# A two-layer hybrid encoder in fp32: the first FFN stage's down projection by seven products, the residual in one tile, and three token tiles added to it by one accumulating DMA

## The chip, the cores and the metric

The kernel is one program on one NeuronCore of a Trainium2 chip. The metric is the device time of one execution in microseconds (us); the median of several runs is given. The profile is one execution seen by the hardware profiler. The engines are TensorE (PE: matmuls; PEld: its weight loads), VectorE (DVE), ScalarE (ACT), GpSimd (POOL) and SyncE (SP, which here only issues DMAs). GpSimd issues DMAs too, on a software queue of its own.

## The reference

Two token sequences (512 and 256 tokens, together 768 = 6 tiles of 128, model width 1024) go through two layers. Each layer has a half-step SwiGLU FFN, a mixer, and a second half-step FFN:

```python
def swiglu(x, wg, wu, wd):
    return (jax.nn.silu(x @ wg) * (x @ wu)) @ wd
...
x = x + 0.5 * swiglu(rms_norm(x, norm_ffn[layer, 0]), w_ffn_gate[layer, 0],
                     w_ffn_up[layer, 0], w_ffn_down[layer, 0])
hn = rms_norm(x, norm_mix[layer])
# even layer: z = hn @ w_in_even, a state-space scan and neighbourhood attention, @ w_out_even
# odd layer:  z = hn @ w_in_odd, windowed grouped attention, @ w_out_odd
x = x + 0.5 * swiglu(rms_norm(x, norm_ffn[layer, 1]), ...)
```

The FFN's inner width is 2816 = 22 chunks of 128. All data are fp32. The result is `rms_norm(x, norm_final)` of both sequences.

## The kernel before

The program has six stages in a row: FFN 0 (until about 565 us), the even mixer (until 890), FFN 1 (until 1383), FFN 2 (until 1875), the odd mixer (until 2150) and FFN 3. The residual x lives in SBUF all along, in six tiles of 128 tokens x 1024 (`self.x`).

**Precision.** Each fp32 matrix is held as a high and a low part; a product is the three matmuls high x high, high x low and low x high. A weight tile `raw` comes by a DMA of SP (L80); ScalarE casts its high part (L89), VectorE subtracts it to get the low part (L90), both into a tile `whl`, of which there are seven.

**An FFN stage.** The 22 chunks are taken in 11 pairs b. For a pair, gate and up projections are done over a 2 x 2 split (two chunks, two halves of the tokens) by seven products of sub-matrices and sums of them instead of eight (Strassen and Winograd); each product is 12 matmuls of 128x384 (`prod`, L283). Beside block b, the down projection of block b-1 is woven in (`woven`). In stages 1 to 3 it goes by seven products too (`down`): 7 x 9 matmuls of 128x512 (L391), each giving three token tiles of one 512-wide half of x. Six of seven products are evacuated by ScalarE into a tile y (L398) and added to x by an accumulating DMA that GpSimd issues (L399), one for each token tile; the product of quadrant (1,0), and one tile more, are added by VectorE (L395). In stage 0 the down projection is `plain`: 12 steps of 6 matmuls (L469), added to x by VectorE (L416). The last block of every stage is plain (`step`, L457), and there the next norm begins, token tile by token tile (L217 to L232, transposes L1269).

**Sums for the seven products.** In stages 1 to 3 the hidden tiles `h` are also combined to s1 to s4, each with a cast on ScalarE and a subtraction on VectorE. Stage 0 needs none of them (`last` is true there for every block).

**The state-space preparation** runs beside stage 0 (`extra`, one step after each product from block 2 on): it turns the scan's parameters into matrices in DRAM (W1d, W2d, Ed) for the even mixer. First VectorE works out powers (L558 to L655). Then there are 16 rounds, one for each pair of groups: `start` runs a chain of some 20 GpSimd operations (L677 to L700), `finish` stores W2 (L706), transposes w1 on TensorE (four transposes, L711, and small matmuls, L718 to L722), ScalarE copies the transposed tile to `w1e` (L712), and `store` writes it to W1d (L729) and a small tile to Ed (L730). The chain's scratch (n1, n2, m1, m2) lies in the same memory as `w1e`, so the next chain's first operation (L677) waits until the store to W1d has landed. At the end SP gathers Md from Ed (L744).

All instructions of an engine run in program order, as do the DMAs of one queue; the framework sets semaphore waits where tiles overlap.

Of the kernel before, what the change touches and what calls it, by code (L numbers as in the profile page):

```python
# [12 lines left out]
F32 = mybir.dt.float32  # L13
F32R = mybir.dt.float32r
I32 = mybir.dt.int32
AF = mybir.ActivationFunctionType
ALU = mybir.AluOpType
# [3 lines left out]
P = 128  # L21
# [26 lines left out]
class Trunk:  # L48
    def __init__(self, ctx, tc, a, y_p, y_s):
# [12 lines left out]
        self.one = warm  # L62
        self.x = [self.xp.tile([P, DM], F32, name=f"x{t}", tag=f"x{t}") for t in range(6)]
        self.queue = deque()
# [33 lines left out]
    def weights(self):  # L98
# [62 lines left out]
        def fast(q):  # L161
            both = ("w_gate", "w_up")
            first = [quad(n, q, 0) for n in both]
            for z in first * 2 + [head(n, q, 1) for n in both] * 2 + first * 5:
                yield next(z)
            for b in range(1, NF // 2):
                pair = [quad(n, q, b, b == 1) for n in both]
                if q == 0:
                    yield from chain(pair[0], plain(q, b - 1), pair[1])
                else:  # L170
                    yield from woven(b, chain(*pair), down(q, b - 1))
            yield from plain(q, NF // 2 - 1)
# [85 lines left out]
    def ffn(self, q, norm, tail, extra=None):  # L258
# [5 lines left out]
        with ExitStack() as ctx:  # L264
# [9 lines left out]
            def ct():  # L274
                return fp.tile([P, H], F32, tag="ct", name="ct", bufs=5)

# [70 lines left out]
            def up(b):  # L347

                last = b == NF // 2 - 1 or q == 0
                sums = {}  # L350
# [28 lines left out]
            def down(b):  # L379
# [4 lines left out]
                def step(h, w, bank, first, i, j):  # L384
                    w = self.take("w_down", q, b, w)
                    for n in range(3):
                        if first:
                            z[bank, n] = self.ps()
                        o = z[bank, n]
                        for m, (a, c) in enumerate(((0, 0), (1, 0), (0, 1))):  # L390
                            nc.tensor.matmul(o, hs[h][:, c, n * P : (n + 1) * P], w[:, a], start=first and m == 0, stop=m == 2,  # L391
                                             skip_group_check=True)
                        xs = self.x[TILES[3 * i + n]][:, j * 512 : (j + 1) * 512]
                        if (i, j) == (1, 0) or (i, j, n) == (0, 0, 0):
                            v.scalar_tensor_tensor(xs, o, 0.5, xs, ALU.mult, ALU.add)  # L395
                        else:
                            y = fp.tile([P, 512], F32, tag="y", name="y", bufs=5)
                            nc.scalar.activation(y, o, AF.Copy, scale=0.5)  # L398
                            nc.gpsimd.dma_start(xs, y, accum_op=ALU.add)  # L399

# [3 lines left out]
                    ("s4", "22", "c", False, 0, 1))]  # L404

            def plain(b):

                st = {}

                def step(e, n):  # L410
                    if n == 0:
                        st["w"] = [self.take("w_down", q, 2 * b + f, e) for f in range(2)]
                    o = self.ps()
                    self.rows(o, act, n, st["w"])
                    xs = self.x[TILES[n]][:, e * 512 : (e + 1) * 512]
                    v.scalar_tensor_tensor(xs, o, 0.5, xs, ALU.mult, ALU.add)  # L416

                return [lambda e=e, n=n: step(e, n) for e in range(2) for n in range(6)]

# [17 lines left out]
            for b in range(1, NF // 2):  # L437
                g, u = (z[2:] for z in (g1, u1)) if b == 1 else pair(b)
                for s in g + plain(b - 1) + u if q == 0 else woven(b, g + u, iter(down(b - 1))):
                    s()  # L440
                    if b > 1:
                        next(extra, None)
# [73 lines left out]
    def s5_matrices(self, pool, spare):  # L516
# [148 lines left out]
        def start(q):  # L665
# [10 lines left out]
            for r in range(2):  # L676
                gp.tensor_mul(n1[:, r], b[:, r], crb)  # L677
                gp.tensor_mul(n2[:, r], b[:, 1 - r], cib)
            yield
            gp.tensor_sub(bb[:, 0, :2], n1[:, 0], n2[:, 0])  # L680
# [19 lines left out]
            gp.tensor_add(w1[:, :, 1], m1, m2)  # L700
            yield

# [739 lines left out]
```

## Time and profile before

| | before |
|---|---|
| median of 3 runs | 2641.98 us (2640.18 to 2642.34) |
| the profiled execution's own time | 2640.13 us |
| its span in the trace | 2638.3 us |
| busy share of the span: PE, DVE, ACT, POOL | 98%, 76%, 59%, 29% |
| moved by DMA | 342.92 MB, mean 130 GB/s |

A busy share is that of the whole span and mixes stages with different limits. The span is what the trace covers; the run's own time is 1.8 us longer, and the median of the other runs 1.85 us above that.

### The profile page before, as it was taken

Reading aid. Unit: us, or ns where it says so; the run is one execution under the profiler, and the core shown is the slowest. Engines: PE = TensorE matmul, PEld = TensorE weight load, DVE = VectorE, ACT = ScalarE, POOL = GpSimd, SP = SyncE. Lnnn points to the kernel's source line nnn. Section 1 sums busy time; section 2 is a strip of 40 time slices with the busy share of each in tenths; the row PEclk is TensorE's granted clock in tenths of the full one; section 3 lists DMA queues with packets and bytes.
Section 4 is the critical chain, followed back from the end, with each engine's and each line's share of the span. In section 5 each row is a group of like instructions: output and inputs, shape, how many; then the busy total and the mean of one; then the engine's idle time right before and its main releaser. Section 6 shows DMA issues by size and latency. Waiting matters only on the chain.

```text
span 2638.3 us, 40405 instructions
## 1 busy us (share of the span) xinstructions
PE 2595.2 (98%) x14370; PEld 2344.0 (89%) x14370; DVE 2015.5 (76%) x3925; ACT 1545.2 (59%) x3202; POOL 769.1 (29%) x1191
## 2 busy tenths in 40 slices
PE   8999999999999999999999999999999999999998
PEld 7999899888787899999998999999887789999997
DVE  8977777564864888787879878787647788878786
ACT  6334334354564666666667666666558766666665
POOL 0255655302820033333321323232100003333332
PEclk9999999999999999999999999999999999999999
DMA  4223223326243277777755877777401127777775
GB/s 154 71 90 104 78 91 104 106 74 155 82 155 108 88 168 165 171 166 170 167 108 137 190 169 167 168 170 148 128 17 41 65 88 168 165 171 166 170 167 129
DMA packets 145661, 342.92 MB, mean 130 GB/s; under 512 B 25265, under 2 KB 32385, under 8 KB 145202
## 3 DMA queue, kind: packets, MB, share of 16 engines
q0 software_dynamic: 74032, 139.01, 29.3%
q1 hardware_dynamic: 71426, 201.33, 23.7%
q8 instruction: 113, 1.85, 0.3%
q14 instruction: 90, 0.74, 0.1%
HBM read 198.65 MB, written 17.89 MB: 82 GB/s over the span
## 4 chain that ended last, share of the span: by engine, by line
PE 73%; DVE 4%; ACT 2%; DMA 1%; issue 1%; POOL 0%; DVEq 0%; ACTq 0%; POOLq 0%
PE ps L283 33%; PE ps L391 16%; PE ps L255 9%; PE ps L487 5%; PE ps L469 2%; PE ps L1111 1%; DVE whl L90 1%; PE ps L1099 1%; PE ps L1130 1%; DMA x<-y 1%; DVE raw L232 1%; PE ps L920 1%; PE ps L855 1%; PE ps L819 1%; PE ps L883 1%
## 5 line engine op out<-in xcount | busy, mean ns | idle before, releaser
L90 DVE TENSOR_TENSOR whl<-raw,whl 128x512 fp32r<-128x512 f32 x856 | 597.7, 704 | 346.7 <-ACT whl L89 337.1
L283 PE MATMUL ps<-bt,whl 128*128 128x384 f32 x4224 | 784.0, 337 | 14.6 <-ACT ct L315 5.8
L283 PEld LDWEIGHTS ps<-bt,whl 128*128 128x128 f32 x4224 | 742.0, 188 | 34.4 <-ACT ct L315 7.2
L89 ACT CAST whl<-raw 128x512 fp32r<-128x512 f32 x856 | 526.0, 621 | 327.5 <-issue 78.2
L399 POOL DMA_DIRECT2D x<-y x480 | 420.4, 1037 | 1009.9 <-ACT y L398 869.5
L283 PE MATMUL ps<-b,whl 128*128 128x384 f32 x3168 | 586.7, 336 | 3.6 <-ACT b L1294 2.9
L283 PEld LDWEIGHTS ps<-b,whl 128*128 128x128 f32 x3168 | 555.4, 188 | 14.4 <-ACT b L1294 3.3
L398 ACT ACTIVATE y<-ps 128x512 f32<-128x512 f32 x480 | 279.0, 598 | 67.7 <-PE ps L391 26.6
L391 PE MATMUL ps<-whl,hl 128*128 128x512 f32 x1080 | 269.8, 393 | 0.2 <-ACT hl L89 0.2
L391 PEld LDWEIGHTS ps<-whl,hl 128*128 128x128 f32 x1080 | 200.8, 188 | 36.7 <-ACT hl L89 0.5
L255 PE MATMUL ps<-hn,whl 128*128 128x256 f32 (+1 forms) x1248 | 228.7, 340 | 0.7 <-ACT hn L89 0.5
L255 PEld LDWEIGHTS ps<-hn,whl 128*128 128x128 f32 x1248 | 190.9, 190 | 29.3 <-issue 2.2
L391 PE MATMUL ps<-whl,h 128*128 128x512 f32 x810 | 202.9, 394 | 0.0
L469 PE MATMUL ps<-whl,h 128*128 128x512 f32 x756 | 191.1, 392 | 0.0
L391 PEld LDWEIGHTS ps<-whl,h 128*128 128x128 f32 x810 | 150.3, 188 | 28.2 <-ACT y L398 0.5
L469 PEld LDWEIGHTS ps<-whl,h 128*128 128x128 f32 x756 | 140.5, 188 | 30.1 <-ACT h L89 1.0
L89 ACT CAST h<-hct 128x384 fp32r<-128x384 f32 x132 | 67.8, 514 | 125.9 <-DVE hct L354 123.3
L89 ACT CAST whl<-st 128x512 fp32r<-128x512 f32 x118 | 72.8, 617 | 61.4 <-PE ps L469 39.9
L416 DVE SCALAR_TENSOR_TENSOR x<-ps,x 128x512 f32<-128x512 f32 x120 | 80.9, 685 | 34.4 <-PE ps L469 34.4
L395 DVE SCALAR_TENSOR_TENSOR x<-ps,x 128x512 f32<-128x512 f32 x150 | 99.9, 684 | 4.1 <-PE ps L391 4.1
L487 PE MATMUL ps<-whl,ob 128*128 128x512 f32 x432 | 102.5, 392 | 0.0
L90 DVE TENSOR_TENSOR whl<-st,whl 128x512 fp32r<-128x512 f32 x118 | 82.8, 701 | 22.3 <-ACT whl L89 20.8
(263 smaller groups left out, 3306.7 us busy)
## 6 DMA issues: line engine op xcount, KB each, us to landing
x<-y POOLq DMA_DIRECT2D x480, 256.0 KB, 5.2
raw<-in_w_gate SPq DMA_DIRECT2D x92, 512.0 KB, 5.5
raw<-in_w_up SPq DMA_DIRECT2D x92, 512.0 KB, 3.7
raw<-in_w_down SPq DMA_DIRECT2D x88, 512.0 KB, 5.3
raw<-in_w_in_even SPq DMA_DIRECT2D x16, 512.0 KB, 3.6
raw<-in_w_in_odd SPq DMA_DIRECT2D x10, 512.0 KB, 6.5
W2d<-raw POOLq DMA_DIRECT2D x16, 256.0 KB, 2.9
W1d<-hct POOLq DMA_DIRECT2D x16, 256.0 KB, 2.4
```

The source lines that it names most:

```text
L89: nc.scalar.copy(hl, src)
L90: nc.vector.tensor_sub(lo, src, hl.bitcast(F32))
L232: nc.vector.scalar_tensor_tensor(out[:, c], self.x[t][:, c], ss[:, 0:1], gb[:, c], ALU.mult, ALU.mult)
L255: self.nc.tensor.matmul(o, w[k // 4][:, j, k % 4 * P : (k % 4 + 1) * P], act[i][k // 4][:, k % 4, k0 : k0 + n], start=k == 0 and (j, i) == ...
L283: nc.tensor.matmul(o, w[:, j, k * P : (k + 1) * P], B[z][:, i, k], start=first and k == 0 and (j, i) == (0, 0), stop=k == 3 and (j, i) == ...
L391: nc.tensor.matmul(o, hs[h][:, c, n * P : (n + 1) * P], w[:, a], start=first and m == 0, stop=m == 2, skip_group_check=True)
L395: v.scalar_tensor_tensor(xs, o, 0.5, xs, ALU.mult, ALU.add)
L398: nc.scalar.activation(y, o, AF.Copy, scale=0.5)
L399: nc.gpsimd.dma_start(xs, y, accum_op=ALU.add)
L416: v.scalar_tensor_tensor(xs, o, 0.5, xs, ALU.mult, ALU.add)
L469: self.nc.tensor.matmul(o, act(f, i, n), w[:, j], start=f == 0 and (j, i) == (0, 0), stop=f == 1 and (j, i) == (0, 1))
L487: nc.tensor.matmul(o, act(i, k)[:, t * P : (t + 1) * P], st["w"][k][:, j], start=m == 0, stop=m == 11)
```

## The change

The first stage's blocks 1 to 10 call `down` like the other stages, so `plain` as a block step and its branch go, and `last` is true only in the last block. The residual becomes one tile `self.X` of 128 x 6 x 1024 with the six token tiles as views. In `down`, a product's three token tiles are copied by ScalarE into one tile y of 128 x 3 x 512 (two buffers; before, five of 128x512) and added to x by one DMA; all three tiles of quadrant (1,0) go by VectorE, and no other. The first stage has four ct buffers instead of five. In the preparation two of the eight `yield`s of a round's `start` go, so that a round has fewer steps.

```diff
-        self.x = [self.xp.tile([P, DM], F32, name=f"x{t}", tag=f"x{t}") for t in range(6)]
+        self.X = self.xp.tile([P, 6, DM], F32, name="x", tag="x")
+        self.x = [self.X[:, TILES.index(t)] for t in range(6)]
...
-                return fp.tile([P, H], F32, tag="ct", name="ct", bufs=5)
+                return fp.tile([P, H], F32, tag="ct", name="ct", bufs=5 if q else 4)
...
-                last = b == NF // 2 - 1 or q == 0
+                last = b == NF // 2 - 1
...
                 def step(h, w, bank, first, i, j):
                     w = self.take("w_down", q, b, w)
+                    direct = (i, j) == (1, 0)
+                    if not direct:
+                        y = fp.tile([P, 3, 512], F32, tag="y", name="y", bufs=2)
                     for n in range(3):
...
-                        xs = self.x[TILES[3 * i + n]][:, j * 512 : (j + 1) * 512]
-                        if (i, j) == (1, 0) or (i, j, n) == (0, 0, 0):
+                        if direct:
+                            xs = self.X[:, 3 * i + n, j * 512 : (j + 1) * 512]
                             v.scalar_tensor_tensor(xs, o, 0.5, xs, ALU.mult, ALU.add)
                         else:
-                            y = fp.tile([P, 512], F32, tag="y", name="y", bufs=5)
-                            nc.scalar.activation(y, o, AF.Copy, scale=0.5)
-                            nc.gpsimd.dma_start(xs, y, accum_op=ALU.add)
+                            nc.scalar.activation(y[:, n], o, AF.Copy, scale=0.5)
+                    if not direct:
+                        nc.gpsimd.dma_start(self.X[:, 3 * i : 3 * i + 3, j * 512 : (j + 1) * 512], y, accum_op=ALU.add)
...
-                for s in g + plain(b - 1) + u if q == 0 else woven(b, g + u, iter(down(b - 1))):
+                for s in woven(b, g + u, iter(down(b - 1))):
                     s()
                     if b > 1:
                         next(extra, None)
...
                 gp.tensor_mul(n2[:, r], b[:, 1 - r], cib)
-            yield
             gp.tensor_sub(bb[:, 0, :2], n1[:, 0], n2[:, 0])
...
             gp.tensor_add(w1[:, :, 1], m1, m2)
-            yield
```

The order in which instructions stand on an engine follows from the order of emission. On GpSimd (POOL) this is the end of one round of the preparation and the start of the next, before the change; `DMA W1d` is the round's store, and its wait is for ScalarE's copy:

```order
L706 DMA W2d<-raw 128x512
L696 TENSOR_TENSOR raw<-hct 128x2x128 [waits Pool_49]
L697 TENSOR_TENSOR hct<-s5k,raw 128x256 [waits Pool_49]
L699 TENSOR_TENSOR hct<-s5k,raw 128x256
L700 TENSOR_TENSOR raw<-hct 128x2x128 [waits Pool_49]
L729 DMA W1d<-hct 128x512 [waits Activation_49]
L663 DMA s5k<-in_s_bc 128x128 [waits PE_49]
L682 TENSOR_SCALAR s5k<-s5k 128x32 [waits DMASW6_49,PE_49]
L730 DMA Ed<-hct 64x240 [waits DMASW3_49,DVE_49,Activation_49]
L677 TENSOR_TENSOR hct<-s5k 128x32 [waits DMASW1_49,Pool_49]
```

After the change the end of the round that follows (lines up to L691 are 15 lower) has three transfers of y to x between the chain's last operation (L686) and the store; in the round before this one, one such transfer stands between L691 and L682, and two between L686 and L714:

```order
L691 DMA W2d<-raw 128x512 [waits DMASW5_49]
L682 TENSOR_TENSOR raw<-hct 128x2x128 [waits Pool_49]
L683 TENSOR_TENSOR hct<-s5k,raw 128x256 [waits Pool_49]
L685 TENSOR_TENSOR hct<-s5k,raw 128x256
L686 TENSOR_TENSOR raw<-hct 128x2x128 [waits Pool_49]
L400 DMA x<-y 128x3x512 [waits DMASW7_49,Activation_49]
L400 DMA x<-y 128x3x512 [waits DMASW1_49,Activation_49]
L400 DMA x<-y 128x3x512 [waits DMASW0_49,Activation_49]
L650 DMA s5k<-in_s_bc 128x128 [waits PE_49]
L714 DMA W1d<-hct 128x512 [waits Activation_49]
```

The transfers of y, which GpSimd did not have in this stage, now stand between the chain and the store; each waits for ScalarE's copies and for one earlier transfer.

On SP, near the end of the first stage, these are the loads before the change; one weight load waits for GpSimd (`Pool_49`):

```order
L80 DMA raw<-in_w_up 128x1024 [waits DMAHW0_49,DVE_49]
L80 DMA raw<-in_w_up 128x1024 [waits Pool_49]
L80 DMA raw<-in_w_down 128x1024 [waits DMAHW1_49,DVE_49]
L80 DMA raw<-in_w_down 128x1024 [waits DMAHW2_49,DVE_49]
L247 DMA raw<-in_norm_mix 128x1024 [waits DMAHW3_49,DVE_49]
L80 DMA raw<-in_w_in_even 128x1024 [waits DMAHW4_49,DVE_49]
```

and after it:

```order
L81 DMA raw<-in_w_up 128x1024 [waits DMAHW1_49,DVE_49]
L81 DMA raw<-in_w_down 128x1024 [waits DMAHW4_49,DVE_49]
L81 DMA raw<-in_w_down 128x1024 [waits DMAHW2_49,DVE_49]
L245 DMA raw<-in_norm_mix 128x1024 [waits Pool_49]
L81 DMA raw<-in_w_in_even 128x1024 [waits DMAHW5_49,DVE_49]
```

The wait for GpSimd has moved from a load of an up weight to that of the mixer's norm gain.

On VectorE, in the third block of the first stage, this is the end of the preparation's powers after the change (`raw`, `hct` of 32 columns and of 512 on 64 partitions are theirs); L91 is the low part of a weight tile or of h:

```order
L633 TENSOR_SCALAR hct<-raw 128x32
L636 COPY raw<-raw 64x512
L637 COPY raw<-raw 64x512
L396 SCALAR_TENSOR_TENSOR x<-ps,x 128x512 x2
L304 TENSOR_TENSOR hct<-ps,hct 128x384
L142 TENSOR_TENSOR st<-raw 128x512
L352 TENSOR_TENSOR hct<-hct 128x384
L145 TENSOR_TENSOR raw<-raw 128x512
L146 TENSOR_TENSOR raw<-st,raw 128x512
L91 TENSOR_TENSOR h_214<-hct,h_214 128x384
L151 TENSOR_TENSOR raw<-raw 128x512
L91 TENSOR_TENSOR whl<-raw,whl 128x512
```

The weight tile before that of the last row stands 64 rows above it; between them are small operations of the preparation, for the most part, and the rows shown.

## Rows read from the trace of the kernel before

**Rows 1.** The page: busy time, share of the span and instructions of each engine.

```profile
PE 2595.2 (98%) x14370; PEld 2344.0 (89%) x14370; DVE 2015.5 (76%) x3925; ACT 1545.2 (59%) x3202; POOL 769.1 (29%) x1191
```

**Rows 2.** Windows: stretch, us; busy PE, PEld, DVE, ACT, POOL; granted clock, DMA share, GB/s.

```profile
130.00:540.00 410.00, 404.15 (x2446) 372.30 (x2446) 296.76 (x448) 153.72 (x314) 209.22 (x346) 0.99 0.28 93
934.00:1360.00 426.00, 425.87 (x2236) 397.60 (x2235) 339.79 (x577) 275.32 (x532) 138.25 (x158) 1.00 0.78 168
```

**Rows 3.** Timeline of PE in FFN 1: start, us, what, number.

```profile
1004.62 2.24 PE L391 MATMUL ps<-whl,hl 128*128 128x512 f32 x9
1006.70 2.27 PE L283 MATMUL ps<-bt,whl 128*128 128x384 f32 x12
1008.80 2.24 PE L283 MATMUL ps<-b,whl 128*128 128x384 f32 x12
```

**Rows 4.** Timeline of PE late in FFN 0; in brackets idle time and releaser.

```profile
504.51 3.94 PE L283 MATMUL ps<-bt,whl 128*128 128x384 f32 x12 [5.84 <-ACT ct L315]
```

**Rows 5.** Waits of SP's queue, 470 to 640: sum us, times, longest.

```profile
SPq L80 <- POOL hct L699: 20.4, 1, 20.4
```

**Rows 6.** Waits, 130 to 560: sum us, times, longest.

```profile
POOL W1d L729 <- ACT hct L724: 90.7, 8, 18.8
POOL W1d L729 <- ACT hct L712: 67.9, 8, 12.6
```

**Rows 7.** Timeline of POOL in FFN 0: two chains and a store.

```profile
290.62 0.24 POOL L677 TENSOR_TENSOR hct<-s5k 128x32 f32<-128x32 f32 x1 [0.31 <-DMA W1d<-hct]
...
303.56 1.10 POOL L700 TENSOR_TENSOR raw<-hct 128x256 f32<-128x256 f32 x1
...
315.20 0.58 POOL L729 DMA_DIRECT2D W1d<-hct  x1 [10.55 <-ACT hct L724]
...
318.10 0.24 POOL L677 TENSOR_TENSOR hct<-s5k 128x32 f32<-128x32 f32 x1 [0.78 <-DMA W1d<-hct]
...
328.20 0.74 POOL L700 TENSOR_TENSOR raw<-hct 128x256 f32<-128x256 f32 x1
```

**Rows 8.** Line L399, windows 1004 to 1008, then 1000 to 1004: issues, landings.

```profile
L399 POOL DMA_DIRECT2D x<-y x3: 854/1197/1501, 1006.8 to 1007.9; - x3
...
DMA to landing us min/median/max: 3.4/4.3/5.1
...
L399 POOL DMA_DIRECT2D x<-y x3: 862/1167/1456, 1000.4 to 1001.6; - x3
...
DMA to landing us min/median/max: 5.3/6.0/6.7
```

**Rows 9.** Timeline at the end of FFN 1.

```profile
1358.08 0.60 ACT L398 ACTIVATE y<-ps 128x512 f32<-128x512 f32 x1
...
1362.34 1.29 DVE L457 SCALAR_TENSOR_TENSOR x<-ps,x 128x512 f32<-128x512 f32 x2 [0.59 <-PE ps L469]
...
1365.03 1.28 DVE L232 SCALAR_TENSOR_TENSOR raw<-x,ss,raw 128x1024 f32<-128x1024 f32 x1
...
1368.06 1.03 PE L1269 MATMUL ps<-ident,raw 128*128 128x128 f32 x8
```

**Rows 10.** Timeline of PE in FFN 0: the transposes of one round, the next product.

```profile
140.86 0.60 PE L711 MATMUL ps<-ident,raw 128*128 128x128 f32 x4
...
142.16 4.43 PE L283 MATMUL ps<-bt,whl 128*128 128x384 f32 x24
```

**Rows 11.** Timeline of DVE in FFN 0, the end of the powers.

```profile
112.12 0.23 DVE L635 TENSOR_TENSOR raw<-hct 128x64 f32<-128x64 f32 x1
...
114.28 0.69 DVE L90 TENSOR_TENSOR whl<-raw,whl 128x512 fp32r<-128x512 f32 x1
114.89 0.17 DVE L645 COPY hct<-raw 128x32 f32<-128x32 f32 x1
114.98 0.17 DVE L646 TENSOR_SCALAR hct<-raw 128x32 f32<-128x32 f32 x1
```

**Rows 12.** Lines by form: number, busy us, mean ns, idle time before, releasers.

```profile
L399 POOL DMA_DIRECT2D x<-y x480 | 420.4, 1037 | 1009.9 <-ACT y L398 869.5 <-DVE bt L1298 89.2 <-ACT h L89 32.0
```

More of the change, by code (lines that the diff above doesn't have):

```diff
@@ L167, in fast @@
                 pair = [quad(n, q, b, b == 1) for n in both]
[L168 to L171, printed above, removed]
+                yield from woven(b, chain(*pair), down(q, b - 1))
             yield from plain(q, NF // 2 - 1)
@@ L404, in down @@
                     ("s4", "22", "c", False, 0, 1))]
[L406 to L418, printed above, removed]
             def pair(b):
```

## The prediction

> **What bounds the kernel now.** I read the first lines of the page, then the busy time by stage, then TensorE's own rows. TensorE is busy 98% of the span and no other engine over 76% [rows 1]; in the second FFN stage it is busy 425.87 of 426 us, in the first 404.15 of 410, both at a granted clock of 0.99 to 1.00 [rows 2]. So time falls only where matmuls go or where TensorE stands still, and rises where something that TensorE waits for comes late. Beside that, the first stage carries a second program: the state-space preparation, 16 rounds of one GpSimd chain, four transposes and some small matmuls on TensorE, and a store. GpSimd is busy 209.22 of 410 us there, against 138.25 of 426 in the second stage, where it issues the y transfers alone [rows 2]; after the change the first stage holds both. There lies the risk.
>
> **Matmuls that go.** Ten of the first stage's eleven blocks lose 72 - 63 = 9 matmuls of 128x512. Nine of them run from 1004.62 to 1006.70, where the next product begins: 2.08 us, 0.231 each [rows 3]. 10 x 9 x 0.231 = **20.8 us**. TensorE's clock has nothing to give back here, being full already [rows 2].
>
> **A stall that goes.** TensorE stands 5.84 us at 504.51, for a ct that waits for a late evacuation [rows 4]; ahead of it one weight load had waited 20.4 us on the SP queue for GpSimd to be done with a buffer [rows 5]. In the changed order the load that waits there for GpSimd is a norm's gain row, which only the stage's end needs. **-5.8** (bounds -5.8 and 0: another load may take its place).
>
> **The preparation's loop.** This is the term that decides. Before, GpSimd ends its chain early and idles 90.7 + 67.9 us in 16 waits for ScalarE's copy behind the transposes [rows 6], 9.9 us a round. The changed order puts three y transfers between the chain's last operation and that store in every other round; in the rounds between, one stands inside the chain and two behind it (both in the section on the change). GpSimd takes its instructions in order, so a y whose product TensorE finished long ago is issued when the chain ends. There are two y buffers, so the evacuation of product k+2 waits until product k's transfer has landed. The store W1d follows the last y on the same software queue, and the next chain's first operation waits for W1d to land, since it writes the same scratch; before, W1d's way from issue (315.20) to that operation (318.10) was 2.9 us [rows 7].
>
> The durations: a chain runs from 290.62 to 304.66 = 14.0 us, the next from 318.10 to 328.94 = 10.8 [rows 7]; mean 12.4. The trace has no transfer of three tiles. Its nearest rows are three of one tile issued in a row: in one group the issues start between 1006.8 and 1007.9 and land 3.4, 4.3 and 5.1 us later, in another they start between 1000.4 and 1001.6 and land 5.3, 6.0 and 6.7 later [rows 8]. So the third tile is there 1.1 + 5.1 = 6.2 us after the first issue, or 1.2 + 6.7 = 7.9; the tiles come 1.4 and 1.3 apart. I take the middle, 7.0, with 6.2 and 7.9 as bounds. The three ScalarE copies take 3 x 0.6 = 1.8 [rows 9]. W1d is one tile of 256 KB behind the y; I take 1.0 for it, between nothing and the 2.9 that it takes alone, near the 1.3 to 1.4 between tiles but without the read of what it adds to.
>
> - Round with three y behind the chain: first y lands 7.0, copies 1.8, last y lands 7.0, W1d 1.0, next chain 12.4 = **29.2 us**.
> - Round with one y inside the chain, issued some 3.3 us (four operations of about 0.8) before its end: 29.2 - 3.3 = **25.9 us**.
> - TensorE's own round: eleven products of 2.09 [rows 3] and 1.3 for the transposes and small matmuls, which run from 140.86 to 142.16 [rows 10] = **24.3 us**.
>
> The rounds alternate: mean 27.55, 3.25 over TensorE's. Over 15 rounds that is 49 us, of which GpSimd's present lead of 9.9 us absorbs the start: 39. With a landing of 6.2 the rounds are 27.6 and 24.3, 1.65 over: 25 - 10 = 15. I take the middle of the two, **+27**. The bounds: landing 6.2 with a chain of 10.8 gives 26.0 and 22.7, 0.05 over, which the lead covers (0); landing 7.9 with 14.0 gives 32.6 and 29.3, 6.65 over, 100 - 10 = 90.
>
> The Trainium skill's page "DMA: Bandwidth & Descriptors", section "Anatomy of one DMA — SWDGE (gpsimd) path", gives such a transfer about 2.0 us plus its bytes over 436 KB/us; for 768 KB that is an estimate of 3.8 us, and the rounds would be 22.8 and 19.5, below TensorE's 24.3, with no stall at all. The single tile speaks against it: 256 KB would be 2.6 us by that rule, where the quickest of six took 3.4 [rows 8].
>
> **VectorE in the first blocks.** While the preparation's powers are worked out, VectorE is full of small operations. In the changed order 29 operations of 128x32, 21 of 128x64 and 16 of 384 or 512 columns stand between two weight tiles of the third block. Starts are 0.09 us apart for the first kind and 0.61 for the longest, and one of the second takes 0.23 [rows 11]: 29 x 0.09 + 21 x 0.23 + 16 x 0.61 = 17.2 us. TensorE has at most seven weight tiles ready ahead, 7 x 2.09 = 14.6 us. **+3** (0 to 6). Later a block of the first stage costs VectorE what it costs in the second stage, 339.79 / 426 = 80% [rows 2], and one small operation a round for the preparation; ScalarE, 275.32 / 426 = 65%, and three small copies. Both stay below TensorE: **0**.
>
> **Evacuation in the other stages.** Six transfers a block in place of sixteen. The 420.4 us that GpSimd spends on issuing them [rows 12] is off the path (it is busy 138.25 of 426 us there [rows 2]). Whether a transfer of three tiles costs it one y's 1.04 us or three times that [rows 12], nothing waits for it: with two buffers a product's copy waits for the transfer two before it, and products of `down` come 6.3 us apart (two others of 2.09 lie between), so a landing of 6.2 to 7.9 and 1.8 of copies are over before the 12.5 us that separate product k from k+2. **0.** That cover is gone where the two exceed 12.5 us: each us above is then 1 us in ScalarE's queue, which casts TensorE's weights.
>
> **Stage ends.** In the second stage the last copy ends at 1358.68 and x is next added to at 1362.34 [rows 9]. Three tiles that land 6.2 to 7.9 after the copy are there at 1364.9 to 1366.6, 2.5 to 4.2 late. The norm's row that this feeds is ready at 1366.31 and TensorE's transposes begin at 1368.06 [rows 9], so 1.75 of it is slack: +0.8 to +2.5 at each of three ends, 1.4 taken, and 2.6 at the program's end, where nothing hides it: **+7** (0 to 12).
>
> **Sum,** on the profiled execution's own 2640.13 us: -20.8 - 5.8 + 27 + 3 + 7 = +10.4, so 2650.5. The median of the runs is 2641.98, 1.85 above; the forecast is **2652 us**. A change under 0.2% (5.3 us) cannot be told from none.
>
> **Rivals.**
> 1. *The loop has room; the matmuls decide.* Landing 6.2 and a chain of 10.8: the loop adds 0, and 2640.1 - 26.6 + 10 + 1.9 = **2625 us**, with the other two terms at zero 2615. For it: 9.9 us of GpSimd's wait a round [rows 6], and the shorter of the two chains. Against it: the first y stands behind the chain whatever its length, and lands before the third can be copied. It decides where the mean round is below 25.8 us (15 x 1.5 - 10 = 12). This is the other side. Chance 0.36. The Trainium skill's fit above leads here too.
> 2. *Both cancel:* a loop of 12 to 22 us, 2637 to 2647. Chance 0.14.
> 3. *The loop is longer:* chain of 14.0 as VectorE, busier than before, and GpSimd slow each other, as a 14.0 beside a 10.8 suggests [rows 7]; landing 7.9: +55 to +90, **2680 to 2715 us**. Against it: the DMA share in the first stage is 0.28 before, against 0.78 where the y rows were read [rows 2]. Chance 0.12, within slower.
> 4. *The transfer of three tiles waits for all of x,* as x is one tile now, and so does VectorE's direct add: the copies would then wait in all stages, and TensorE with them, one landing of 7 us a block over 40 blocks, +280. The changed order shows waits for single transfers two places back alone, and VectorE's direct add waits for TensorE alone. Chance 0.01.
>
> The forecast's own case (a loop of 22 to 55, 2647 to 2680) has 0.37. Faster 0.36, same 0.14, slower 0.50. The range leaves out 1 in 10 on each side: **2616 to 2692**.
>
> **What would show it.** Right: in the changed profile TensorE's small-matmul groups follow one another at about 27 us on the mean and not 24.3, TensorE waits at the transposes or for weights held up by ScalarE, ScalarE's y waits for a landing, GpSimd's first operation of a chain for W1d; GpSimd's 158 us of waits for ScalarE's copy are gone; three tiles land in about 7 us. The first stage ends some 5 us later than now, and the stages behind keep their lengths within 3 us each. Wrong: landing near 5, no wait for W1d, rounds of 24.3 us, and the first stage some 20 us shorter. The prediction falls first by the landing of three tiles, which no row shows.

## The result, and the profile after

The changed kernel takes 2730.39 us (median of 4 runs, 2728.45 to 2732.3) against 2642.15 for the kernel before: ratio 1.0335, 95% interval 1.0323 to 1.0348, 88 us slower. The forecast was 2652, with 2616 to 2692 as its range: the side was right and the size was not.

The page after, in the same order as [rows 1] (busy time and share), then one row of the costly groups and two of the DMA issues (bytes, median us to landing):

```profile
span 2730.3 us, 39956 instructions
...
PE 2609.9 (96%) x14280; PEld 2347.0 (86%) x14280; DVE 2024.3 (74%) x3915; ACT 1677.4 (61%) x3502; POOL 681.1 (25%) x951
...
L398 ACT ACTIVATE y<-ps 128x512 f32<-128x512 f32 x720 | 404.7, 598 | 119.5 <-DMA x<-y 91.4
...
x<-y POOLq DMA_DIRECT2D x240, 768.0 KB, 7.9
...
W1d<-hct POOLq DMA_DIRECT2D x16, 256.0 KB, 8.5
```

90 matmuls went, as worked out (14370 to 14280). Of the 92.0 us that the span is longer (2638.3 to 2730.3), TensorE stands 77.3; in the other 14.7 it is busy, although it has fewer matmuls: the granted clock is lower for part of them, as the windows below show. The rows of ScalarE and of the store point at the waits: 91.4 us of ScalarE's idle time before its copies to y end when a y transfer has landed, and the store W1d lands 8.5 us after its issue, where the page before has 2.4:

```profile
W1d<-hct POOLq DMA_DIRECT2D x16, 256.0 KB, 2.4
```

Where on the way? TensorE's transposes of the first mixer's norm begin at 632.77 in place of 553.14 (the first row is of the kernel before):

```profile
553.14 1.03 PE L1269 MATMUL ps<-ident,raw 128*128 128x128 f32 x8
...
632.77 1.94 PE L1254 MATMUL ps<-ident,raw 128*128 128x128 f32 x8 [3.14 <-DVE raw L230]
```

So 79.6 us are lost in the first stage. From there to the end it takes 2097.5 us in place of 2085.2, 12.4 more. The windows of the preparation's rounds and of the second FFN stage, to be held against [rows 2]:

```profile
150.00:610.00 460.00, 397.23 (x2259) 353.78 (x2260) 321.45 (x468) 238.46 (x493) 293.18 (x391) 0.94 0.69 154
1010.00:1440.00 430.00, 430.00 (x2264) 402.67 (x2263) 333.64 (x567) 285.84 (x560) 75.19 (x59) 1.00 0.85 179
```

In the rounds TensorE stands 63 of 460 us, and the clock that it is granted is 0.94 on average. In the second stage, with the same blocks and the same y transfers but no preparation, it never stands. The 16 groups of transposes lie at 151.36 to 609.15, so a round is 30.5 us on average, where the forecast had 27.55 and TensorE's own work 24.3. 15 x (30.5 - 24.3) = 93 us. The first group and the last:

```profile
151.36 0.60 PE L696 MATMUL ps<-ident,raw 128*128 128x128 f32 x4
...
609.15 0.60 PE L696 MATMUL ps<-ident,raw 128*128 128x128 f32 x4
```

What a round is made of shows in the chain of work that ended last, here between 380 and 425 us (start, us, what):

```profile
389.24 0.92 POOL raw L686
390.17 7.20 DMA x<-y
...
397.47 0.18 ACT y L398
...
398.98 1.00 ACT y L398 x2
...
400.40 1.28 POOL x L400
...
401.85 9.49 DMA W1d<-hct
...
411.48 0.23 POOL hct L664
```

No TensorE stands in it. The chain's last operation (L686) ends, the first y behind it goes out and lands 7.20 us later; only then may ScalarE copy the next product but one into the freed buffer; its transfer is issued at 400.40, the store W1d behind it at 401.85, and when that has landed the next chain may begin at 411.48. This is the loop of the prediction, piece by piece, in one of its longest rounds. The chain ahead of it began at 374.06, 37.4 us before the next:

```profile
374.06 1.05 POOL L664 TENSOR_TENSOR hct<-s5k 128x32 f32<-128x32 f32 x1 [8.97 <-DMA W1d<-hct]
...
390.17 2.59 POOL L400 DMA_DIRECT2D x<-y  x2
400.40 1.28 POOL L400 DMA_DIRECT2D x<-y  x1 [7.64 <-ACT y L398]
401.85 0.62 POOL L714 DMA_DIRECT2D W1d<-hct  x1 [0.16 <-issue]
```

The waits of 130 to 620 (sum us, times, longest) say the same of all rounds:

```profile
ACT y L398 <- DMA x<-y: 82.1, 16, 11.7
DVE whl L91 <- ACT whl L90: 71.9, 49, 8.6
POOL x L400 <- ACT y L398: 61.4, 14, 7.9
POOL hct L664 <- DMA W1d<-hct: 59.0, 13, 9.0
...
PE ps L281 <- DVE ct L325: 22.9, 11, 6.0
...
PE ps L392 <- ACT y L398: 14.8, 10, 5.0
...
PE ps L696 <- POOL raw L686: 13.6, 6, 3.6
...
POOL W1d L714 <- ACT hct L708: 8.8, 6, 2.8
```

The 158.6 us that GpSimd used to idle for ScalarE's copy ahead of the store [rows 6] are down to some 12; instead it waits 59.0 us for the store and 61.4 for ScalarE's copies into y. That TensorE itself waits for the chain's end only 13.6 us does not clear the chain: it stands longer for VectorE's sums (22.9) and for ScalarE's copies out of the products (14.8), and VectorE in turn waits 71.9 us for ScalarE's casts of weights, 8.6 at the longest (before, in 130 to 560: 47.4, and 1.9 at the longest). ScalarE takes its work in order, so casts and copies stand behind its wait for a y buffer. That last step is read from the order and these rows; no run tries it alone.

### The profile page after: what moved, and what is told of

The parts are those of the page before. It is cut to its first block, busy times and chain, and to the rows that moved or that the text cites. A ratio compares the mean times of both kernels' runs of the same rounds, so it can differ in the third digit from the quotient of the medians.

```text
span 2730.3 us, 39956 instructions
## 1 busy us (share of the span) xinstructions
PE 2609.9 (96%) x14280; PEld 2347.0 (86%) x14280; DVE 2024.3 (74%) x3915; ACT 1677.4 (61%) x3502; POOL 681.1 (25%) x951
## 4 chain that ended last, share of the span: by engine, by line
PE 75%; DMA 8%; DVE 7%; POOL 5%; ACT 3%; issue 2%; DVEq 0%; ACTq 0%; POOLq 0%; SPq 0%
PE ps L281 36%; PE ps L392 18%; PE ps L253 9%; PE ps L474 4%; DMA x<-y 3%; DMA W1d<-hct 3%; DVE whl L91 2%; PE ps L1096 1%; DVE raw L230 1%; PE ps L1084 1%; PE ps L456 1%; PE ps L1115 1%; DMA raw<-in_w_up 1%; ACT whl L90 1%; ACT y L398 1%
## 5 line engine op out<-in xcount | busy, mean ns | idle before, releaser
L91 DVE TENSOR_TENSOR whl<-raw,whl 128x512 fp32r<-128x512 f32 x876 | 614.8, 711 | 390.6 <-ACT whl L90 382.3
L281 PE MATMUL ps<-bt,whl 128*128 128x384 f32 x4224 | 796.9, 340 | 39.5 <-DVE ct L325 22.9
L400 POOL DMA_DIRECT2D x<-y x240 | 310.2, 1298 | 1370.4 <-ACT y L398 1191.9
L398 ACT ACTIVATE y<-ps 128x512 f32<-128x512 f32 x720 | 404.7, 598 | 119.5 <-DMA x<-y 91.4
L392 PE MATMUL ps<-whl,hl 128*128 128x512 f32 x1440 | 362.2, 395 | 5.7 <-ACT y L398 5.5
L392 PEld LDWEIGHTS ps<-whl,hl 128*128 128x128 f32 x1440 | 268.7, 189 | 57.3 <-ACT y L398 8.0
L392 PE MATMUL ps<-whl,h 128*128 128x512 f32 x1080 | 275.5, 399 | 9.2 <-ACT y L398 9.2
L392 PEld LDWEIGHTS ps<-whl,h 128*128 128x128 f32 x1080 | 203.3, 191 | 48.9 <-ACT y L398 11.0
L91 DVE TENSOR_TENSOR whl<-st,whl 128x512 fp32r<-128x512 f32 x128 | 92.6, 724 | 9.2 <-ACT whl L90 9.1
L91 DVE TENSOR_TENSOR h<-hct,h 128x384 fp32r<-128x384 f32 x132 | 75.8, 574 | 30.7 <-ACT h L90 30.3
L474 PEld LDWEIGHTS ps<-whl,ob 128*128 128x128 f32 x432 | 80.0, 188 | 18.5 <-issue 1.6
L142 DVE TENSOR_TENSOR st<-raw 128x512 f32<-128x512 f32 x88 | 62.6, 711 | 41.9 <-DMA raw<-in_w_up 28.2
L319 ACT COPY ct<-ps 128x384 f32<-128x384 f32 x88 | 42.4, 482 | 73.3 <-PE ps L281 73.2
```

The source lines that it names most:

```text
L91: nc.vector.tensor_sub(lo, src, hl.bitcast(F32))
L142: v.tensor_add(s1, a21, a22)
L281: nc.tensor.matmul(o, w[:, j, k * P : (k + 1) * P], B[z][:, i, k], start=first and k == 0 and (j, i) == (0, 0), stop=k == 3 and (j, i) == ...
L319: nc.scalar.copy(z["r5"], z["c"])
L398: nc.scalar.activation(y[:, n], o, AF.Copy, scale=0.5)
L400: nc.gpsimd.dma_start(self.X[:, 3 * i : 3 * i + 3, j * 512 : (j + 1) * 512], y, accum_op=ALU.add)
```

## The experiments

Each ratio below is to runs of the kernel before on the same chip.

**Leaving out the chain.** Two kernels, the changed one with GpSimd's arithmetic done in two rounds, then in none:

```diff
+            if q > 1:                      # e_no_chain;  q >= 0 in e_no_chain_all
+                for _ in range(6):
+                    yield
+                return
             for r in range(2):
                 gp.tensor_mul(n1[:, r], b[:, r], crb)
```

> The changed kernel with GpSimd's chain of the preparation worked out for the first two rounds alone; in the other 14 GpSimd does none of its arithmetic, and transposes, copies, stores and loads stay (so the state-space matrices of the later groups are those of the first). Theory L (the loop of chain, y transfers behind it and the store that the next chain waits for sets the first stage's pace): with the chain gone the loop is some 15 us shorter than its 30.5, rounds fall to TensorE's 24.3, and the time to 2625 to 2640 us. Rival S (the sums' added work on VectorE and ScalarE, and two y buffers, are enough to slow the stage): 2710 us or more.

> The changed kernel with GpSimd's chain left out in all 16 rounds, its results set to zero once (so the state-space matrices are zero); the powers on VectorE, transposes, copies, stores and loads stay. With two rounds of the chain left the time was 2650 and rounds 1 to 3 still took 24.4, 32.9 and 28.9 us. If these come from the loop, all rounds are 24.4 and the time is 2634 to 2642 us; if VectorE's small operations in the first blocks make them, 2646 to 2652. The stall in the third block (4.9 us at 136 us, with the clock low behind it) stays in either case.

Measured: 2650.06 us (ratio 1.0031, 1.002 to 1.0042) and 2635.13 us (0.9975, 0.9966 to 0.9984). The first lies 10 us above L's range, the second inside its own. Everything that rival S holds responsible (sums, copies, y transfers, two buffers, the store behind them) is still there in the second, and its rounds are 24.4 us from the third on; two neighbouring groups of transposes on TensorE:

```profile
321.26 0.60 PE L703 MATMUL ps<-ident,raw 128*128 128x128 f32 x4
...
345.64 0.60 PE L703 MATMUL ps<-ident,raw 128*128 128x128 f32 x4
```

So the chain on GpSimd costs 2730 - 2635 = 95 us in this kernel. Two rounds of it alone cost 15 (2650 - 2635): rival S falls. Leaving the chain out takes away two things at once, though: its place in the loop, and what GpSimd's arithmetic does to VectorE, whose subtractions for the weights take 812 ns on average in 200 to 500 beside the chain, and 688 without it:

```profile
L91 DVE TENSOR_TENSOR whl<-raw,whl 128x512 fp32r<-128x512 f32 x93 | 75.3, 812 | 42.7 <-ACT whl L90 42.1
...
L91 DVE TENSOR_TENSOR whl<-raw,whl 128x512 fp32r<-128x512 f32 x117 | 80.2, 688 | 63.8 <-ACT whl L90 63.0
```

VectorE is busy 206 of these 300 us with the chain, so it is not the bound there. The edits at the store, next, leave the arithmetic as it is and change only order and queues.

**The store from another place.** 

```diff
-            nc.scalar.copy(w1e, pt)
+            nc.scalar.copy(w1f, pt)
-            nc.gpsimd.dma_start(self.W1d[:, gs, :], w1e...)
+            nc.gpsimd.dma_start(self.W1d[:, gs, :], w1...)
```

> The changed kernel with one edit: ScalarE copies the transposed tile into w1's own place, and W1d is stored from there, so that the first half of the next chain need not wait for the store. Theory L: the wait of 59 us of GpSimd for W1d in 13 rounds goes for the most part, a round loses 5 to 9 of its 30.5 us, and the time is 2635 to 2670 us. Rival S: no change, 2725 to 2735 us. Rival Y (the y transfers of three tiles and their two buffers are the bound, not the chain): 2715 us or more.

`w1f` is the same memory as `w1`. Measured: 2694.56 us (1.0198, 1.0182 to 1.0213), above L's range. The wait for W1d at a chain's first operation is gone, and a round is 28.1 us: 2.4 shorter, not 5 to 9. Four operations of the next chain now run ahead of the y; the others still stand behind them on GpSimd's queue. The direction is L's, the size is not; rival S's and rival Y's ranges are missed too.

**The store on another queue, and both.**

```diff
-            nc.gpsimd.dma_start(self.W1d[:, gs, :], ...)
+            nc.scalar.dma_start(self.W1d[:, gs, :], ...)
```

> The changed kernel with one edit: the store W1d is issued by ScalarE, which made its data, on a hardware queue, and so no longer stands behind the y transfers on GpSimd's software queue. Theory L with the queue as a part of the loop (the store lands some 9 us after the last y's issue only because the y is ahead of it): GpSimd's 59 us of waits for W1d fall below 20, a round loses 4 to 6 of its 30.5 us, 2640 to 2675 us. If the store is late of itself, or the chain and the y alone make the round: 2710 us or more.

> The changed kernel with both edits: transposed tile copied into w1's own place, and W1d stored by ScalarE's queue. Theory L: GpSimd waits for W1d no more; what is left of the loop is chain, y behind it and its landing (10 us for three y, 15 for the chain, 25 against TensorE's 24.3), 2630 to 2660 us. If it is not below the kernel with ScalarE's store alone, the scratch was no bound of its own.

Measured: 2711.35 us (1.0265, 1.025 to 1.0281) and 2691.55 us (1.0188, 1.0173 to 1.0203), both above what L gave. Waits of the kernel with the store on ScalarE's queue (130 to 590):

```profile
ACT y L398 <- DMA x<-y: 72.6, 17, 11.5
...
POOL hct L664 <- DMA W1d<-hct: 38.3, 13, 6.4
```

The store did stand behind the y on the software queue: on ScalarE's queue it lands 5.6 us after its issue in the median instead of 8.5. But only 21 of the 59 us of waiting went with that. With both edits the wait for the store is gone, and 28.0 us a round are left, with 41.8 us of ScalarE's waits for y buffers. With the scratch free, the store's queue is worth 3 us at most (2694.56 to 2691.55). So the store was one part of the loop; the y on an in-order queue behind a chain is the other, and taking away the one lets the other show.

**Fewer y, other DMAs off GpSimd.** With both edits, four y a block instead of six (VectorE adds quadrant (0,0) too), then the parameters' load and the store to Ed on ScalarE's queue as well:

```diff
-                    direct = (i, j) == (1, 0)
+                    direct = (i, j) == (1, 0) or q == 0 and (i, j) == (0, 0)
...
-            (nc.gpsimd if q > 1 else nc.sync).dma_start(bc[q % 2], a["s5_bc"][q])
+            (nc.scalar if q > 1 else nc.sync).dma_start(bc[q % 2], a["s5_bc"][q])
...
-            nc.gpsimd.dma_start(self.Ed[gs].rearrange("g c n -> (g c) n"), ee)
+            nc.scalar.dma_start(self.Ed[gs].rearrange("g c n -> (g c) n"), ee)
+            if q + 2 < G // 2:
+                load(q + 2)
```

The first line of the diff is in both kernels, the rest in the second alone.

> Both edits, and in the first stage the product of quadrant (0,0) that y took is added by VectorE too, so that four y transfers a block are left instead of six. Theory L: one or two y behind the chain, none waits for another's landing, rounds of 24.3, 2620 to 2640 us, perhaps below the kernel before. Rival V (VectorE, at 80% without this, becomes the bound with 6 more adds a block): above 2660 us.

> Both edits and four y in the first stage (2678 us, rounds of 26.5), and the preparation's other two DMAs of a round, the parameters' load and the store to Ed, issued by ScalarE: GpSimd, whose queue waited 52 us for TensorE to be done with the parameters, is left with the chain, y and W2d. Theory L (in-order GpSimd queue as a whole): rounds near 24.4, 2645 to 2662 us. If VectorE with its added adds holds the rest: 2670 us or more.

Measured: 2677.82 us (1.0139, 1.0124 to 1.0154; rounds of 26.5) and 2667.0 us (1.0098, 1.0084 to 1.0111; rounds of 26.0). Both lie above L's ranges. Every DMA taken from GpSimd's queue gives something, none gives all. GpSimd's longest wait in the first of the two was another in-order one, for TensorE to be done with the parameters:

```profile
POOL s5k L650 <- PE ps L707: 52.2, 11, 8.4
```

The first of the two also meets rival V's mark (above 2660), and V is not excluded here. VectorE, with the added sums and the chain beside it, is busy 260.02 of the 300 us from 200 to 500, and TensorE's stall in the third block is 9.55 us, where the changed kernel has 4.99:

```profile
200.00:500.00 300.00, 284.80 (x1694) 259.85 (x1694) 260.02 (x387) 160.40 (x331) 202.47 (x270) 0.98 0.63 149
...
142.04 1.01 PE L281 MATMUL ps<-bt,whl 128*128 128x384 f32 x2 [9.55 <-ACT whl L90]
```

So the edits to order and queues win back 63 of the 88 us, the added sums against them; how the 32 that are left above the kernel without a chain (2667 - 2635) divide between what is left of the loop and a VectorE that is slower and fuller, no run separates.

**The seven products with single tiles.** The kernel before, with `down` in its first stage, and with the four ct buffers and the two yields fewer of the changed kernel; then with both edits at the store:

```diff
-                for s in g + plain(b - 1) + u if q == 0 else woven(b, g + u, iter(down(b - 1))):
+                for s in woven(b, g + u, iter(down(b - 1))):
```

> The kernel before with the first stage's down projection by seven products alone: x in six tiles, y one token tile each, five buffers, 16 transfers a block. Theory L: the store stands behind the last of several single y in the same way; single tiles land in 4 to 6 us and five buffers hold nearly two products, so rounds of 27 to 29 us, 2670 to 2710 us. Rival Y: with single tiles rounds are 24.3 and the time is 2620 to 2635 us. Rival S: 2710 us or more.

> The kernel before with the first stage by seven products, single y tiles, and both edits at the store. Theory L: 18 single issues of 1.0 us a block and the chain fill GpSimd, rounds of 25 to 27 us, 2635 to 2675 us, near the same kernel with three-tile transfers. If single tiles are better in this stage by themselves: below that kernel by 10 us or more.

Measured: 2706.02 us (1.0239, 1.0222 to 1.0256) and 2680.32 us (1.0144, 1.0127 to 1.0161), rounds of 29.3 and 27.6. The first is in L's range, the second 5 us above it. Five buffers of one tile still lose 65 of the 88 us: rival Y falls as the main cause. The transfer of three tiles takes 24 us of the 88 at most (2730 - 2706), part of it at the stage ends. The second kernel is 11 us below the one with three-tile transfers and both edits, which by its expectation would make single tiles better in this stage by themselves; but in the two traces the first mixer's transposes begin at 590.76 and 593.92, so only 3.2 of it lie in the first stage.

**The other stages alone.** The changed kernel with a plain first stage (and with it the five ct buffers and all the yields of the kernel before), then with the last down block's y in transfers of one tile:

```diff
+                            if b == NF // 2 - 2:
+                                nc.gpsimd.dma_start(self.X[:, 3 * i + n, ...], y[:, n], accum_op=ALU.add)
-                    if not direct:
+                    if not direct and b < NF // 2 - 2:
```

> The changed kernel with the first stage's down projection plain as before: what is left of the change is x in one tile and three token tiles by one transfer in the other three FFN stages. Theory L and S alike: the stage ends wait for the later landing, +1 to +4 us at each of four ends, 2645 to 2655 us. If the other stages paid more than that, above 2660.

> The kernel with a plain first stage, x in one tile and three-tile transfers in the other stages (2646 us, 4.9 above the kernel before), but in the last block of down products of a stage each token tile goes by a transfer of its own. If the later landing of the last three tiles makes the loss, 2640 to 2643 us; if the transfers cost inside the stages, 2645 to 2648.

Measured: 2646.19 us (1.0018, 1.0009 to 1.0027) and 2637.98 us (0.9988, 0.9979 to 0.9997). The end of FFN 1 with the transfer of three tiles:

```profile
1357.47 2.24 PE L395 MATMUL ps<-whl,hl 128*128 128x512 f32 x9
...
1360.96 1.27 POOL L403 DMA_DIRECT2D x<-y  x1 [5.18 <-ACT y L401]
...
1367.51 1.29 DVE L461 SCALAR_TENSOR_TENSOR x<-ps,x 128x512 f32<-128x512 f32 x2 [2.50 <-PE ps L473]
...
1371.01 1.06 PE L1273 MATMUL ps<-ident,raw 128*128 128x128 f32 x8 [0.81 <-DVE raw L233]
```

and with single ones:

```profile
1355.19 2.24 PE L395 MATMUL ps<-whl,hl 128*128 128x512 f32 x9
...
1357.23 2.59 POOL L403 DMA_DIRECT2D x<-y  x3 [3.63 <-ACT y L401]
...
1362.05 1.29 DVE L463 SCALAR_TENSOR_TENSOR x<-ps,x 128x512 f32<-128x512 f32 x2 [0.60 <-PE ps L475]
...
1367.77 1.03 PE L1275 MATMUL ps<-ident,raw 128*128 128x128 f32 x8
```

The same product (L395) begins 2.28 us later in the first trace already, which arose earlier and has to be taken off. What is left: the issue comes 1.45 us later with three tiles, since it waits for the third copy. VectorE's second add to x waits 2.50 us; the row puts that down to TensorE, but the transfer issued at 1360.96 takes 6.5 to 6.8 us to land. And the next norm's transposes begin 0.96 us later. Laid beside the kernel before matmul by matmul, the three-tile kernel loses 2.0 us at the end of FFN 1 and as much at that of FFN 2, and gains about 1 inside each of the two stages; with single tiles at the ends that loss is gone. So there the loss sat at the stage ends. With single tiles at them, x in one tile and fewer transfers inside the stages come out slightly ahead of the kernel before, and 2 us below the range that was expected: this is the fastest kernel of the study that computes everything, by 0.1% with an interval that ends just short of none.

**Seven products where the chain rests.** First every other block (4, 6, 8, 10), on the single-tile kernel with both edits:

> The kernel before with both edits at the store, and the first stage's down projection by seven products in blocks 4, 6, 8 and 10 alone, the others plain, y in single tiles: 4 x 2.08 = 8.3 us of matmuls less, no y in the blocks where the powers are worked out, and each block with y followed by one without, in which the loop catches up. Theory L: 2628 to 2640 us, below the kernel before. If y beside a chain costs more than the next block gives back: 2645 us or more.

```diff
-                for s in woven(b, g + u, iter(down(b - 1))):
+                for s in woven(...) if q or b in (4, 6, 8, 10) else g + plain(b - 1) + u:
```

Measured: 2663.01 us (1.0075, 1.0063 to 1.0088), a miss: it is where the expectation had y beside a chain cost more than the next block gives back. GpSimd here waits 65.7 us for TensorE to be done with the parameters, in ten rounds, at most 14.0 at a time, and the y stand behind that. Whether the edits at the store bring this wait, or the two yields fewer, was not tried (the kernel before without the yields alone waits 34.8 us there, in five rounds), so the loss has no shown cause.

Then the last two blocks alone. The preparation without its two yields ends earlier, which two kernels try by itself:

```diff
-                for s in g + plain(b - 1) + u if q == 0 else woven(...):
+                for s in woven(...) if q or b > 8 else g + plain(b - 1) + u:
```

```diff
                 gp.tensor_mul(n2[:, r], b[:, 1 - r], cib)
-            yield
...
             gp.tensor_add(w1[:, :, 1], m1, m2)
-            yield
```

> The kernel before with nothing changed but the preparation's two yields, which the change takes away: rounds of 11 steps instead of 13, so about 21 us, and the preparation ends some 50 us earlier. GpSimd had 9.9 us of waits a round and keeps about 6. The stall of 5.84 us late in the first stage, whose removal was a term of -5.8: if it hangs on where the preparation ends, 2634 to 2638 us; if a weight load waits for GpSimd's buffer wherever that is, 2640 to 2643. If the chain cannot keep up with 21 us: 2650 or more.

> The kernel with x in one tile, three-tile transfers in the later stages, single ones at the stages' ends and a plain first stage (2638 us), with the two yields taken away: the same -6 to 0 as in the kernel before, 2632 to 2639 us. It is the base of the next kernel.

> That kernel with seven products in the first stage's last two blocks alone (9 and 10), where the preparation is over or nearly so. Theory L (the seven products cost nothing by themselves, only beside the chain): 2 x 2.08 = 4.2 us below the kernel without them, and below both kernels of the change, 2628 to 2636 us. If the sums on VectorE and ScalarE or the y cost more than the matmuls give, even with no chain: above it by 2 us or more.

Measured: 2643.23 us (1.0006, 0.9998 to 1.0015), 2640.56 us (0.9994, 0.9985 to 1.0003) and 2640.77 us (0.9997, 0.9988 to 1.0006); the last two are above their ranges. The yields alone give nothing: TensorE's late stall moves with the preparation's end (7.08 us at 453.43 in place of 5.84 at 504.51) and does not go. And the two blocks of seven products give nothing either, where 4.2 us were expected. (This kernel also has four ct buffers in the first stage, where its base has five.) The late stall shrinks to 3.89 us, but TensorE has a new one:

```profile
508.75 1.01 PE L284 MATMUL ps<-bt,whl 128*128 128x384 f32 x2 [4.30 <-ACT whl L90]
```

Its place follows a stretch of 40 us in which 252 GB/s move (460 to 500, 139 in its base): weights, y and the gather of Md at once. That the load there made the weights late was not tried. So the half of the theory that says the seven products pay where no chain runs is shown for zero chains (2635 against 2642) and not for these two blocks.

## Why the prediction was wrong, step by step

- **Matmuls, -20.8: right.** There are 90 fewer, and with no chain a round is 24.4 us where 24.3 was worked out.
- **The late stall, -5.8: wrong in the changed kernel.** It stands 6.00 us at 590.20, behind an up weight's load as before. The SP order told which load waits for GpSimd; it did not tell that another up load, held up 31.5 us by VectorE's use of its buffer, would be as late.

```profile
590.20 4.21 PE L281 MATMUL ps<-bt,whl 128*128 128x384 f32 x12 [6.00 <-DVE ct L325]
```

- **The loop, +27: right as a mechanism, the mis-sized term.** It cost 93 by the length of the rounds and 95 by leaving the chain out. Two steps of its working failed. First, the length of the round: in the changed kernel the chains end 31.0 us apart on the mean, where the forecast had 27.55, and 15 x 3.47 = 52 us are missing by that. Of the 3.47, 2.4 are the chain, which takes 14.8 us on average behind the first one, where 12.4 was taken. 13 of these 15 chains have one y issue inside, 0.9 us until the next operation begins, for which the working had no time; the rest is slower operations. The other 1.0 lies between a chain's end and the next one's start. Nor do the rounds alternate as the two that the order shows: of the 16, five have three y between chain and store, seven two and four one. Second, the middle with a landing of 6.2, which took off another 12: the landings of y between 130 and 620 are 6.5, 7.7 and 14.2 (least, median, most), so the case that was averaged in did not occur.

  The lead did not fail in the sum. The first chain ends 9.1 us ahead of its transposes and the last 1.6, so 7.5 were spent where 9.9 had been taken off: 27 + 52 + 12 + 2 = 93. But it was no cushion on the way. It was gone at the second group, where TensorE waits 0.63 us for GpSimd (178.04), behind a first chain of 20.6 us (121.7 to 142.3, beside VectorE's powers). And where it came back it did not help: the fifth chain ends 6.7 us ahead of its transposes, and the round that begins with them still takes 30.5 us. So the loop does not reach TensorE at the transposes alone.

```profile
264.37 1.07 POOL L686 TENSOR_TENSOR raw<-hct 128x256 f32<-128x256 f32 x1
...
272.12 0.60 PE L696 MATMUL ps<-ident,raw 128*128 128x128 f32 x4
```

  The round shown further up, of the kind with three y behind the chain, is 16.1 (chain) + 7.2 (first y) + 3.0 (copies) + 11.1 (last y's issue to the next chain's start) = 37.4 us, where the forecast had 12.4 + 7.0 + 1.8 + 8.0 = 29.2. Not tried is the changed kernel with the two yields kept: a round would then have 13 products, 13 x 2.09 + 1.3 = 28.5 us of TensorE's own work as an estimate, and the same loop would be less above it.

The first row is y's landings, the second the store's, between 130 and 620:

```profile
DMA to landing us min/median/max: 6.5/7.7/14.2
...
DMA to landing us min/median/max: 2.8/8.5/11.2
```

The Trainium skill's fit ("DMA: Bandwidth & Descriptors", section "Anatomy of one DMA — SWDGE (gpsimd) path") gave an estimate of 3.8 us for a transfer of three tiles. No landing here is below 6.5; the measurement decides, and rival 1, to which it led, is out.

- **VectorE in the first blocks, +3: right place, too small.** TensorE stands 4.99 us at 135.73 and then runs four matmuls in 1.65 us. In 125 to 150 it is busy 19.26 of 25 us at a granted clock of 0.86: some 5.7 us of standing and, as an estimate, 0.14 x 25 = 3.5 of the lower clock. The forecast had no term for the clock.

```profile
135.73 1.65 PE L281 MATMUL ps<-bt,whl 128*128 128x384 f32 x4 [4.99 <-ACT whl L90]
```

- **Stage ends, +7: right.** 4.9 alone, 8.2 between three tiles and one. In the changed kernel the stages behind the first take 12.4 more, of which 4.4 lie in the first mixer; what makes those was not tried.
- **The sum.** -20.8 + 93 + 9 - 0 = 81 for the first stage against 79.6 measured, and 12.4 behind it, 92 in the span. That the forecast had the right side rests on the loop, whose size was a third of the measured one. Rival 3, "the loop is longer", came nearest, with a chance of 0.12: a chain of 14.0 or more and late landings. Even its 2715 was 15 short.

## What to carry to other kernels

Idle time in front of a wait covers a longer loop once, not once a round: work out the loop of what waits for what, around one whole round and in the order of all rounds, with the time of every issue that the new order puts into a chain, and compare its length with the bound engine's round. Do not average in a case that no row has shown. Work that is put on an in-order queue behind a long chain of another program inherits that chain's latency with all its buffers, and cutting one edge of such a loop gives only the difference to the next longest. A transfer that waits for three parts is late where a stage ends, and here it cost nothing inside the stages without such a chain.

## What the runs showed of the hardware that was not expected

- A transfer of three tiles is cheaper than three: 1.30 us of issue in place of 3 x 1.04, and 7.9 us to landing in place of 5.2 for one.
- After a stall TensorE was granted the lower clock (1.2 instead of 2.4 GHz) for some time: 0.50 in 135 to 140, behind the stall of 4.99 us. Nine matmuls of the changed kernel behind 1.79 us of standing span 3.83 us, where they span 2.24 in the second stage [rows 3]; the grant of 181 to 185 is 0.62:

```profile
135.00:140.00 5.00, 3.52 (x10) 2.99 (x11) 5.00 (x6) 3.74 (x7) 4.92 (x6) 0.50 0.39 96
...
181.16 3.83 PE L392 MATMUL ps<-whl,h 128*128 128x512 f32 x9 [1.79 <-ACT y L398]
```

  Over the rounds the grant is 0.94 in place of 0.99 [rows 2]. The loop sets the length of a round, so the two do not simply add.
- GpSimd's operations of one form vary widely: the chain's first, of 128x32, took 1.05 us at 374.06 and 0.23 at 411.48. What slowed it was not tried.
- VectorE's operations vary with them: the same subtraction of 128x512 takes 688 ns on average without the chain and 812 beside it.
